# Splitting two contraction pairs of the down product before they are spilled, and loading their halves straight into place

## The chip, the cores and the metric

The kernel runs on one core of one Trainium2 chip. The metric is the device time of one execution in microseconds (us), the median of several runs. Engines are named as in the profile: PE is TensorE's matmul, DVE VectorE, ACT ScalarE, POOL GpSimd, and SP is the engine that issues all DMAs, in the order in which they stand in its queue.

## The reference

The model is a trunk of two layers over 1024 tokens of width 1024, in float32. The attention and recurrence half of a layer is not touched here. What matters is the MLP behind it (D_FF is 4096):

```python
        h2 = rms_norm(x, norm2_g[l])
        u = jax.nn.relu(jnp.einsum('bsd,df->bsf', h2, w_up[l]))
        x = x + jnp.einsum('bsf,fd->bsd', u * u, w_down[l])
```

Below, the first product is the up product, the second the down product. The down product contracts over the 4096 columns of u*u.

## The kernel before

PE takes operands in a rounded form of float32, so each operand X is split into a high part (ACT casts it, `split_into` L543 and `group` L595) and a low part (DVE subtracts the high part from X). A product of two operands is then three matmuls: low times high, high times low and high times high. One matmul of 128x512 outputs is the unit of PE's work.

Both products of the MLP use Strassen's scheme in Winograd's form. The hidden width of 4096 is cut into 16 pairs (of 256 columns each). For each pair the scheme needs seven right-hand **forms** (B11, B21, T2, T1, T3, B22, T4, in the order of FORMS, L541), and seven left-hand forms of the weights (A11, A12, S2, S1, S3, S4, A22), which `lhs_forms` (L578) makes from a loaded block `wr` (two buffers): POOL forms the sums (tile `wst`), ACT casts (`whi`) and DVE subtracts (`wlo`). `whi` and `wlo` have two buffers each, so a group of weights is cast only when PE is done with the group before the last.

**Up product.** Pairs 0 and 1 are computed by `up_plain`, before the Strassen forms of the input stand. The pairs 2 to 15 are computed by `up_pair` (L650), 84 matmuls each. The results of a pair (squared ReLUs u11, u12, u21, u22, in tiles `x4` to `x7`, which alternate with the parity of q) are turned into the seven down-product forms by `spill` (L695) and written to the DRAM tensor `us`, 256 KB a form. Three partial results (p1, p6, p5) leave PSUM by copies on ACT (`out`, L656); PE goes on accumulating in the same bank only behind such a copy.

**Down product.** It is worked off in steps (`steps`, L963). The first step takes output block 0 with pairs 0 and 1 (42 matmuls), the second block 1 with pair 0 and block 2 with pairs 0, 1, 2 (84 matmuls), then twelve steps follow that move over four pairs each (step r=0 takes pairs 0 to 3). `fetch` (L923) loads the forms of a pair from `us` into the staging tiles `uf` (4 buffers) and `us` (6 buffers) and splits them into the form tiles. Those form tiles are the ones that held the split input of the up product (`form_tiles`, L548): a form tile comes free when the last up pair, q=15, has gone through that form. After each product the step adds the PSUM bank to the residual `x` on DVE (L735), and for the bank "a" PE goes on only behind this add:

```python
                x = xt[2 * t + i][hf]
                with tc.high_priority():
                    V.tensor_tensor(x, ps[j, bk], x, op=ALU.add)
```

**Around the change.** In the pass q=15 the code loads the residual blocks b=0 to 3 (`load_x`, L931, 8 DMAs), prefetches four forms of pair 0 into `uf`, computes the pair, and then splits and fetches the 14 forms of pairs 0 and 1 (L944 to L950), ahead of q=15's own spill; the residual blocks 4 to 7 follow (L952), into the tiles that q=14 and q=15 have left. A scheduler sets the order of each engine's queue from the dependences, its own estimates and the `high_priority` blocks; the code's order is only its starting point.

Of the kernel before, what the change touches and what calls it, by code (L numbers as in the profile page):

```python
# [11 lines left out]
F32 = mybir.dt.float32  # L12
F32R = mybir.dt.float32r
# [7 lines left out]
P = 128  # L21
# [4 lines left out]
HALF = 512  # L26
NH = 4
FF = 4096
NF = FF // P
# [8 lines left out]
LAST = 2 * NH - 1  # L38
US = 6
UF = 4  # L40


@with_exitstack
def trunk(ctx, tc, x, norm1_g, w_in, lam_qk, attn_norm_g, lb_logits, hgrn_norm_g,
# [4 lines left out]
    dma = nc.sync.dma_start  # L49
# [15 lines left out]
    def half(pool, tag, bufs):  # L65
        return pool.tile([P, HALF], F32, tag=tag, name=tag, bufs=bufs)
# [471 lines left out]


    us = dram.tile([P, NF // 2, 7, HALF], F32, name="us")  # L540
    FORMS = ("B11", "B21", "T2", "T1", "T3", "B22", "T4")  # L541

    def split_into(hl, src):  # L543
        A.copy(hl[0], src)
        V.tensor_tensor(hl[1], src, hl[0].bitcast(F32), op=ALU.subtract)
        return hl

    def form_tiles(f, k, mp):  # L548
        if f == "B11":
            return h_tiles(k, 0)  # L550
        if f == "B21":
            return h_tiles(k + 4, 0)
        if f == "B22":
            return h_tiles(k + 4, 1)
        if f == "T1":
            return h_tiles(k, 1)
        return tuple(mp.tile([P, HALF], F32R, tag=f"{f}{k}{i}", name=f"{f}{k}{i}") for i in range(2))
# [137 lines left out]
    def spill(q, u, mp):  # L695
        u11, u12, u21, u22 = u
        t1, t2, t4 = (half(mp, "us", US) for _ in range(3))
        put = lambda f, t: dma(us[:, q, FORMS.index(f)], t)
        put("B11", u11)
        V.tensor_tensor(t1, u12, u11, op=ALU.subtract)  # L700
        put("T1", t1)
        put("B22", u22)
        V.tensor_tensor(t2, u22, t1, op=ALU.subtract)
        put("T2", t2)
        V.tensor_tensor(u12, u22, u12, op=ALU.subtract)
        put("T3", u12)
        put("B21", u21)
        V.tensor_tensor(t4, u21, t2, op=ALU.subtract)
        put("T4", t4)

    def fetch_rhs(q, mp, r, st, names, tag):

        for f in names:
            if st is not None:
                st[f] = half(mp, tag, UF if tag == "uf" else US)
                dma(st[f], us[:, q, FORMS.index(f)])

    def split_rhs(q, mp, r, st):
        for f in list(st):
            r[f] = split_into(form_tiles(f, q % 4, mp), st.pop(f))  # L720
# [35 lines left out]
    for l in range(DEPTH):  # L756
# [7 lines left out]
        for h in range(NH):  # L764
# [35 lines left out]
            st = {}  # L800
# [133 lines left out]
                dma(xt[b][hf], xs[:, b, hf * HALF:(hf + 1) * HALF])  # L934

        for q in range(2, NF // 2):
            if q == NF // 2 - 1:
                for b in range(4):
                    load_x(b)
                st = {}  # L940
                fetch_rhs(0, mp, None, st, FORMS[:UF], "uf")
            u2 = up_pair(up_forms(q, "AS2"), hB, q, xtile, mp)
            if q == NF // 2 - 1:
                for i in range(2):  # L944
                    uB[i] = {}
                    split_rhs(i, mp, uB[i], st)
                    fetch_rhs(i, mp, None, st, [f for f in FORMS if f not in uB[i]][:UF], "uf")
                    split_rhs(i, mp, uB[i], st)
                    if i == 0:
                        fetch_rhs(1, mp, None, st, FORMS[:UF], "uf")  # L950
            spill(q, u2, mp)
        for b in range(4, NB):  # L952
            load_x(b)
# [1 line left out]
        def down_forms(windows, parts):  # L955
            srcs = []
            for t, q0, n in windows:
                src = w_down[l][q0 * 256:(q0 + n) * 256, t * 256:t * 256 + 256]
                srcs.append(src.rearrange("(b p) d -> p b d", p=P))
            return lhs_forms(srcs, mp, "p (j i) c -> p i j c", parts)  # L960


# [54 lines left out]
```

## Time and profile before

| what | value |
|---|---|
| median of 3 runs | 2603.7 us (2601.36 to 2609.66) |
| profiled execution | 2602.21 us, its span 2600.2 us (2.0 us lie around the span) |
| PE busy | 2476.9 us, 95% of the span |
| DVE, ACT, POOL busy | 1837.1 (71%), 1260.4 (48%), 568.5 us (22%) |
| DMA | 306.86 MB, a mean of 118 GB/s; 0.4 to 0.5 of the 16 DMA engines busy in the MLP |

The span holds two layers; the MLP of the first lies from about 640 to 1265 us, that of the second from about 1930 to 2560 us. PE is nearly always busy, so what matters is where it is not: the stretches of a few us in which PE waits. The profile names for each such wait the engine that ended it.

### The profile page before, as it was taken

What the parts mean: (1) busy time and instruction counts of PE and PEld (TensorE: products, weight loads), DVE (VectorE), ACT (ScalarE), POOL (GpSimd) and SP (SyncE); (2) the same over time, 40 slices, a digit from 0 to 9 for tenths busy, and PEclk for the clock granted to TensorE, in tenths of its full rate; (3) what the DMA queues carried; (4) which work ended last, traced back from release to release, by engine and by line L of the source; (5) the groups of instructions that cost most, each with busy time, mean ns of one, the idle gap of its engine ahead of it and who ended that gap; (6) DMA issues with size and microseconds to landing.
All of it is one profiled execution on the core that took longest, in us unless ns stands there. A gap on an engine that the chain in (4) does not pass through costs nothing. (4 is left out here: it accounts for less than half of the span.)

```text
span 2600.2 us, 34936 instructions
## 1 busy us (share of the span) xinstructions
PE 2476.9 (95%) x12688; PEld 2053.2 (79%) x12688; DVE 1837.1 (71%) x3201; ACT 1260.4 (48%) x2439; POOL 568.5 (22%) x328
## 2 busy tenths in 40 slices
PE   8999999999999999999899999999999999899995
PEld 6877887777888877888688778877778888678874
DVE  5567756878756679877745875588786665887865
ACT  6455445654555554443434554456545555533422
POOL 1111011001133323333221111110012333233322
PEclk9999999999999999999999999999999999999998
DMA  7121111245444466453411111111645444754422
GB/s 228 52 61 45 46 37 53 74 141 176 154 154 150 142 214 199 147 162 97 154 49 49 41 37 53 50 41 58 218 129 173 153 155 142 251 159 147 156 85 89
DMA packets 255885, 306.86 MB, mean 118 GB/s; under 512 B 13968, under 2 KB 166844, under 8 KB 255712
## 3 DMA queue, kind: packets, MB, share of 16 engines
q1 hardware_dynamic: 255712, 304.63, 36.1%
q8 instruction: 100, 1.64, 0.3%
q14 instruction: 73, 0.60, 0.1%
HBM read 213.33 MB, written 89.41 MB: 116 GB/s over the span
## 5 line engine op out<-in xcount | busy, mean ns | idle before, releaser
L647 PE MATMUL pa<-T,whi 128*128 128x512 f32 x1456 | 459.1, 396 | 17.4 <-DVE x L735 12.1
L144 PE MATMUL mm<-hh,wlo 128*128 128x512 f32 x896 | 360.1, 402 | 1.7 <-POOL wlo L130 1.7
L144 PE MATMUL mm<-hh,whi 128*128 128x512 f32 x896 | 359.8, 402 | 1.0 <-DVE ta L772 0.9
L144 PE MATMUL mm<-hl,whi 128*128 128x512 f32 x896 | 359.2, 401 | 0.6 <-DVE hl L121 0.5
L647 PEld LDWEIGHTS pa<-T,whi 128*128 128x128 f32 x1456 | 273.1, 189 | 86.4 <-DVE x L735 7.5
L130 POOL TENSOR_TENSOR wlo<-wst,whi 128x1024 fp32r<-128x1024 f32 x56 | 138.9, 2480 | 807.1 <-ACT whi L128 771.4
L620 POOL TENSOR_TENSOR wst<-wr 128x512 f32<-128x512 f32 (+1 forms) x56 | 100.9, 1801 | 914.5 <-DMA wr<-w_down 293.6
L647 PE MATMUL pa<-T,wlo 128*128 128x512 f32 x728 | 287.0, 394 | 0.0
L606 ACT CAST whi<-wst 128x1024 fp32r<-128x1024 f32 (+1 forms) x124 | 127.1, 1025 | 175.8 <-PE mm L647 88.6
L607 DVE TENSOR_TENSOR wlo<-wst,whi 128x1024 fp32r<-128x1024 f32 (+1 forms) x124 | 192.7, 1554 | 14.9 <-ACT whi L606 14.6
L144 PEld LDWEIGHTS mm<-hh,wlo 128*128 128x128 f32 x896 | 170.6, 190 | 36.1 <-POOL wlo L130 4.0
L144 PEld LDWEIGHTS mm<-hl,whi 128*128 128x128 f32 x896 | 171.4, 191 | 33.6 <-DVE hl L121 1.7
L606 ACT CAST whi<-wr 128x512 fp32r<-128x512 f32 (+2 forms) x128 | 105.1, 821 | 189.4 <-PE pr L647 134.7
L144 PEld LDWEIGHTS mm<-hh,whi 128*128 128x128 f32 x896 | 170.7, 191 | 32.8 <-DVE ta L772 1.7
L647 PE MATMUL pr<-hh,whi 128*128 128x512 f32 x480 | 191.7, 400 | 3.6 <-ACT whi L606 3.1
L647 PE MATMUL pr<-hh,wlo 128*128 128x512 f32 x480 | 189.9, 396 | 0.9 <-DVE wlo L607 0.9
L647 PE MATMUL pr<-hl,whi 128*128 128x512 f32 x480 | 188.8, 393 | 0.0
L607 DVE TENSOR_TENSOR wlo<-wr,whi 128x512 fp32r<-128x512 f32 (+2 forms) x128 | 120.9, 945 | 86.3 <-ACT whi L606 84.2
L647 PEld LDWEIGHTS pa<-T,wlo 128*128 128x128 f32 x728 | 137.4, 189 | 33.2 <-DVE wlo L607 0.5
L512 ACT ACTIVATE s<-s,nm 128x256 f32<-128x256 f32 (+7 forms) x128 | 99.0, 774 | 109.2 <-DVE nm L507 105.0
L222 PE MATMUL mm<-wlo,hh 128*128 128x256 f32 x512 | 146.7, 287 | 0.3 <-POOL wlo L130 0.3
L222 PE MATMUL mm<-whi,hh 128*128 128x256 f32 x512 | 147.0, 287 | 0.0
(273 smaller groups left out, 5713.1 us busy)
## 6 DMA issues: line engine op xcount, KB each, us to landing
us<-us SPq DMA_DIRECT2D x216, 256.0 KB, 2.6
wr<-w_up SPq DMA_DIRECT2D x32, 1024.0 KB, 8.3
wst<-w_in SPq DMA_DIRECT2D x56, 512.0 KB, 3.7
uf<-us SPq DMA_DIRECT2D x112, 256.0 KB, 3.1
us<-x SPq DMA_DIRECT2D x112, 256.0 KB, 2.4
wr<-w_down SPq DMA_DIRECT2D x28, 1024.0 KB, 7.8
wst<-w_out SPq DMA_DIRECT2D x32, 512.0 KB, 4.7
x<-xs SPq DMA_DIRECT2D x64, 256.0 KB, 3.7
```

Of the source, the lines that this page charges most:

```text
L130: eng.tensor_tensor(lo, st, hi.bitcast(F32), op=ALU.subtract)
L144: T.matmul(ps, lt[:, b], rt, start=(i == 0), stop=(i == n - 1))
L222: T.matmul(ps[:, t * 256:t * 256 + 256], lt[:, tsl], rt[:, b], start=(i + t + b + k == 0), stop=(i == 1 and b == 3 and k == 2), skip_group ...
L512: A.activation(s[:, :nk], s[:, :nk], AF.Exp, bias=nm, scale=-1.0, accum_out=sm)
L606: A.copy(hv, x)
L607: V.tensor_tensor(lv, x, hv.bitcast(F32), op=ALU.subtract)
L620: G.tensor_tensor(sa[:, 0], a21, a22, op=ALU.add)
L647: T.matmul(ps, lt[:, off + j], rt, start=(start and j + i == 0), stop=(j == n - 1 and i == 2), skip_group_check=True)
```

## The change

- The pairs get **places**: pair q takes place (q - 2) mod 16 in the down product. So the down product begins with the pairs that `up_pair` computes first (q=2 and q=3, places 0 and 1), and the plain pairs 0 and 1 come last. `down_forms` loads the rows of `w_down` to match; where a window straddles the seam, it loads two pieces.
- For places 0 and 1 `spill` splits each form at once, into two `uf` tiles, and writes both halves to a new DRAM tensor `uss` (28 DMAs of 256 KB in place of 14).
- In the pass q=15 these 28 halves are loaded from `uss` straight into the form tiles; the prefetch into `uf` and the 14 splits there are gone.
- `load_x` for blocks 0 to 3 is written in the pass q=8 instead of q=15.

```diff
+READY = 2
...
     us = dram.tile([P, NF // 2, 7, HALF], F32, name="us")
+    uss = dram.tile([P, READY, 7, 2, HALF], F32, name="uss")
+
+    place = lambda q: (q - 2) % (NF // 2)
...
     def spill(q, u, mp):
         u11, u12, u21, u22 = u
         t1, t2, t4 = (half(mp, "us", US) for _ in range(3))
-        put = lambda f, t: dma(us[:, q, FORMS.index(f)], t)
+        p = place(q)
+
+        def put(f, t):
+            if p >= READY:
+                dma(us[:, p, FORMS.index(f)], t)
+                return
+            hl = [half(mp, "uf", UF) for _ in range(2)]
+            split_into([i.bitcast(F32R) for i in hl], t)
+            for i in range(2):
+                dma(uss[:, p, FORMS.index(f), i], hl[i])
+
         put("B11", u11)
...
         for q in range(2, NF // 2):
-            if q == NF // 2 - 1:
+            if q == 8:
                 for b in range(4):
                     load_x(b)
-                st = {}
-                fetch_rhs(0, mp, None, st, FORMS[:UF], "uf")
             u2 = up_pair(up_forms(q, "AS2"), hB, q, xtile, mp)
             if q == NF // 2 - 1:
-                for i in range(2):
+                for i in range(READY):
                     uB[i] = {}
-                    split_rhs(i, mp, uB[i], st)
-                    fetch_rhs(i, mp, None, st, [f for f in FORMS if f not in uB[i]][:UF], "uf")
-                    split_rhs(i, mp, uB[i], st)
-                    if i == 0:
-                        fetch_rhs(1, mp, None, st, FORMS[:UF], "uf")
+                for j, f in enumerate(FORMS):
+                    for i in range(READY):
+                        uB[i][f] = form_tiles(f, i, mp)
+                        for k in range(2):
+                            dma(uB[i][f][k].bitcast(F32), uss[:, i, j, k])
             spill(q, u2, mp)
...
             for t, q0, n in windows:
-                src = w_down[l][q0 * 256:(q0 + n) * 256, t * 256:t * 256 + 256]
-                srcs.append(src.rearrange("(b p) d -> p b d", p=P))
+                cut = min(n, max(NF // 2 - 2 - q0, 0))
+                for p0, m in ((q0, cut), (q0 + cut, n - cut)):
+                    if m:
+                        q = (p0 + 2) % (NF // 2)
+                        src = w_down[l][q * 256:(q + m) * 256, t * 256:t * 256 + 256]
+                        srcs.append(src.rearrange("(b p) d -> p b d", p=P))
```

The scheduler turns this into other queues at three places. Line numbers and tile numbers in what follows are each kernel's own.

**SP, start of the down product.** This is SP's queue from the weights of step r=0 (`wr`, 8x256) to the first load that fetches pair 2 into a `us` tile (B11; in the first layer). Before:

```order
L586 DMA wr_9222<-w_down 128x8x256
L698 DMA us_470<-x5_1_8720 128x512
L934 DMA x7_1_8931<-xs_111 128x512
L716 DMA uf_9039<-us_470 128x512
L716 DMA uf_9186<-us_470 128x512
L934 DMA x5_1_8923<-xs_111 128x512
L716 DMA us_9009<-us_470 128x512
```

After, the same queue from the last `uss` load of form B22 on (T4 is `T400` to `T411`):

```order
L962 DMA hl5_1_8935<-uss_471 128x512
L590 DMA wr_9265<-w_down 128x8x256
L962 DMA T400_8938<-uss_471 128x512
L962 DMA T401_8939<-uss_471 128x512
L962 DMA T410_8942<-uss_471 128x512
L962 DMA T411_8943<-uss_471 128x512
L706 DMA us_470<-x4_1_8782 128x512
L706 DMA us_470<-us_8946 128x512
L706 DMA us_470<-x7_1_8785 128x512
L706 DMA us_470<-us_8947 128x512
L706 DMA us_470<-x5_1_8783 128x512
L706 DMA us_470<-x6_1_8784 128x512
```

Then come the last spill of q=15 (`us_8948`), the eight residual loads of blocks 4 to 7, and only then B11 of pair 2:

```order
L706 DMA us_470<-us_8948 128x512
L948 DMA x4_0_8960<-xs_111 128x512
L948 DMA x4_1_8962<-xs_111 128x512
L948 DMA x5_0_8964<-xs_111 128x512
L948 DMA x5_1_8966<-xs_111 128x512
L948 DMA x6_0_8968<-xs_111 128x512
L948 DMA x6_1_8970<-xs_111 128x512
L948 DMA x7_0_8972<-xs_111 128x512
L948 DMA x7_1_8974<-xs_111 128x512
L730 DMA us_9052<-us_470 128x512
```

Between the weights of r=0 and pair 2's B11 stood 5 DMAs before; now there are 19: T4 of pairs 0 and 1 (4), the whole spill of q=15 (7) and the residual (8).

**PE, from step 1 to step 2.** Before, T4 of pairs 0 and 1 is the last product of step 1 (bank 8957), and step 2 begins behind it (banks 9076, 9079, 9077):

```order
L647 MATMUL pa_8957<-T410_8899,whi_8953 128x512
L647 MATMUL pa_8957<-T411_8900,whi_8953 128x512
L647 MATMUL pa_8957<-T410_8899,wlo_8954 128x512
L647 MATMUL pa_9076<-hh0_0_8827,whi_9054 128x512
L647 MATMUL pa_9076<-hl0_0_8828,whi_9054 128x512
```

After, T4 stands among the first products of step 2 (bank 9000 is step 1's), and ahead of B11 of pair 2 (`hh2_0`) lie pair 2's T1 and other forms that come from `uf`:

```order
L651 MATMUL pa_9000<-T411_8943,whi_8996 128x512
L651 MATMUL pa_9000<-T410_8942,wlo_8997 128x512
L651 MATMUL mm_9123<-hh6_0_9060,whi_9097 128x512
L651 MATMUL mm_9123<-hl6_0_9061,whi_9097 128x512
L651 MATMUL mm_9123<-hh6_0_9060,wlo_9098 128x512
L651 MATMUL pa_9119<-T200_8906,whi_9105 128x512
L651 MATMUL pa_9119<-T201_8907,whi_9105 128x512
```

From the first matmul of step 2 to B11 of pair 2 PE now has 42 matmuls (six of them T4), and from there to step r=0 another 48.

**SP, start of the up pairs.** Before, between the residual loads and the next weights (`wr`), with the prefetch of pair 0 into `uf`:

```order
L934 DMA x3_1_8685<-xs_111 128x512
L716 DMA uf_8687<-us_470 128x512
L698 DMA us_470<-x4_0_6797 128x512
L716 DMA uf_8689<-us_470 128x512
L716 DMA uf_8691<-us_470 128x512
L586 DMA wr_7065<-w_up 128x8x256
```

After, at the same place:

```order
L948 DMA x3_1_7734<-xs_111 128x512
L711 DMA uss_471<-uf_6909 128x512
L711 DMA uss_471<-uf_6910 128x512
L590 DMA wr_7136<-w_up 128x8x256
L711 DMA uss_471<-uf_6916 128x512
L711 DMA uss_471<-uf_6922 128x512
```

The eight loads of the residual blocks 0 to 3 (the last is `x3_1`) stand at the same place in both queues, ahead of the first spill of q=2; the spills of q=2 and q=3 go to `uss` in halves.

## Rows read from the trace of the kernel before

**Rows 1.** Page, head and part 1: span, and each engine's busy time.
```profile
span 2600.2 us, 34936 instructions
PE 2476.9 (95%) x12688; PEld 2053.2 (79%) x12688; DVE 1837.1 (71%) x3201; ACT 1260.4 (48%) x2439; POOL 568.5 (22%) x328
```

**Rows 2.** Timeline of PE, layer 0: start, length, instruction [idle before <- who ended it].
```profile
954.99 0.40 PE L647 MATMUL pa<-hh,whi 128*128 128x512 f32 x1
...
960.02 0.71 PE L647 MATMUL pa<-T,whi 128*128 128x512 f32 x2 [2.10 <-DVE x L735]
...
964.14 0.79 PE L647 MATMUL pa<-T,whi 128*128 128x512 f32 x1 [1.24 <-DVE T L545]
...
979.13 0.50 PE L647 MATMUL mm<-hl,whi 128*128 128x512 f32 x1 [1.91 <-DVE hl L545]
...
994.14 0.40 PE L647 MATMUL pa<-hh,whi 128*128 128x512 f32 x1
...
1007.33 0.71 PE L647 MATMUL pa<-T,whi 128*128 128x512 f32 x2 [2.00 <-DVE x L735]
```

**Rows 3.** The same view, layer 1: steps 1 and r=0 begin, waits in r=0.
```profile
2231.99 0.40 PE L647 MATMUL pa<-hh,whi 128*128 128x512 f32 x1
...
2272.87 0.40 PE L647 MATMUL pa<-hh,whi 128*128 128x512 f32 x1
...
2278.88 0.71 PE L647 MATMUL pa<-T,whi 128*128 128x512 f32 x2 [0.36 <-DVE x L735]
...
2285.86 0.70 PE L647 MATMUL pa<-T,whi 128*128 128x512 f32 x2 [1.22 <-DVE x L735]
```

**Rows 4.** Stretches: length, busy (x count) of PE, PEld, DVE, ACT, POOL, PEclk, DMA, GB/s.
```profile
704.00:724.00 20.00, 20.00 (x88) 16.31 (x88) 12.65 (x12) 10.87 (x16) 7.01 (x6) 1.00 0.42 145
960.00:965.00 5.00, 3.74 (x10) 2.42 (x11) 5.00 (x6) 0.28 (x1) 2.99 (x2) 0.62 0.48 164
2560.00:2565.00 5.00, 4.55 (x20) 4.16 (x21) 2.86 (x9) 1.10 (x3) 1.27 (x1) 0.50 0.08 30
606.00:612.00 6.00, 6.00 (x29) 4.95 (x28) 6.00 (x10) 3.73 (x6) 0.00 (x0) 1.00 1.01 329
688.00:692.00 4.00, 4.00 (x19) 3.11 (x18) 3.24 (x5) 1.54 (x2) 0.00 (x0) 1.00 1.02 380
```

**Rows 5.** Timeline of SP: weights of step r=0, in layer 0 and layer 1.
```profile
967.34 0.38 SPq L586 DMA_DIRECT2D wr<-w_down  x1
...
2243.67 0.38 SPq L586 DMA_DIRECT2D wr<-w_down  x1
```

**Rows 6.** Timelines of DVE and ACT, layer 0: step 1's last weights; first cast from `us`.
```profile
966.86 0.41 DVE L607 TENSOR_TENSOR wlo<-wr,whi 128x256 fp32r<-128x256 f32 x1
...
978.78 0.62 ACT L544 CAST hh<-us 128x512 fp32r<-128x512 f32 x1 [1.78 <-DMA us<-us]
```

**Rows 7.** Instructions on tile `us` (ns min/median/max); weights' cast and DMA landing, from the page.
```profile
L544 ACT CAST T<-us x84: 613/618/627, 983.7 to 2505.1; 128x512 fp32r<-128x512 f32 x84
L545 DVE TENSOR_TENSOR T<-us,T x84: 676/692/1810, 985.8 to 2506.4; 128x512 fp32r<-128x512 f32 x84
L606 ACT CAST whi<-wst 128x1024 fp32r<-128x1024 f32 (+1 forms) x124 | 127.1, 1025 | 175.8 <-PE mm L647 88.6
us<-us SPq DMA_DIRECT2D x216, 256.0 KB, 2.6
```

**Rows 8.** Timeline of PE at the kernel's end: a long wait.
```profile
2559.54 1.86 PE L195 MATMUL pa<-ones,us 128*128 128x1 f32 x8 [11.30 <-DVE us L187]
```

**Rows 9.** Timeline of SP, layer 0: the first residual loads, first and last line of 8 loads.
```profile
667.81 4.17 SPq L934 DMA_DIRECT2D x<-xs  x4
...
690.82 0.54 SPq L934 DMA_DIRECT2D x<-xs  x1
```

**Rows 10.** Pair q=3 in the up product: ACT's copy of p6, PE's next use of that bank.
```profile
712.28 0.59 ACT L659 COPY us<-pa 128x512 f32<-128x512 f32 x1 [0.67 <-PE pa L647]
...
714.85 0.63 PE L647 MATMUL pa<-T,whi 128*128 128x512 f32 x2
```

## The prediction

> **What bounds the kernel now.** First the page's head: PE is busy for 2476.9 of 2600.2 us [rows 1], so only a stretch in which PE waits can give time back, and any new wait of PE is paid in full. Then the timeline of PE, searched for entries with an idle time. The up product has none (from 704 to 724 us PE is busy for 20.00 of 20 [rows 4]); they lie in a cluster at the passage to the down product. There I measure from the start of step 1, T0 = 954.99 us in layer 0 and 2231.99 in layer 1. Step r=0 begins at 994.14 and 2272.87 [rows 2, 3], that is T0+39.2 and T0+40.9. Steps 1 and 2 are 126 matmuls; at full clock PE does 88 in 20.00 us [rows 4], 0.227 us each, so 28.6 us would do. The passage thus loses 10.6 and 12.3 us, and r=0 another 2.00 and 0.36 + 1.22 us [rows 2, 3]. About 26 us in all is what the change can win at most.
>
> Who ends the waits? The first (2.10 us) and those of r=0 are ended by DVE's add of a bank to the residual; the next (1.24 and 1.91 us) by DVE's low parts of right-hand forms [rows 2]. Part of the loss is the clock: from 960 to 965 the granted clock is 0.62 [rows 4].
>
> **What the change takes away.** 28 operations at each passage: 14 casts of 0.62 us on ACT and 14 subtractions of 0.69 us on DVE [rows 7]. DVE's 9.7 us lie in the stretch where DVE ends PE's waits, so 1.24 and 1.91 us can go in layer 0. The first wait stays: the order keeps q=15's own subtractions and step 1's low parts ahead of the first add, and only one split goes from before it. I leave it at 4.6 to 5.0 us after T0.
>
> **What it adds in the up product.** The 28 split operations come back in the passes q=3 and q=4, about 4.3 us of ACT and 4.8 of DVE in each pair's 19.3 us. DVE is busy for 12.65 and ACT for 10.87 of 20 us there [rows 4], so they fit. The risk is order: a form goes through two of four `uf` tiles, so each cast waits on ACT for the landing of the form two before (2.6 us from issue [rows 7]), and ACT's copy of p6 stands behind such casts. The copy ends at 712.87 and PE takes the bank at 714.85 [rows 10], 1.98 us of cover. Going through ACT's new order with the durations of rows 7, the copy ends about 1.7 us later: just covered. I charge 0.25 us for each of four pairs, 1.0 in all (bounds 0 and 12). The 14 more writes per layer, 0.7 us each, fall where the DMA share is 0.42 [rows 4] and cost nothing; without that cover they would cost up to 10 us a layer. The five more pieces of `w_down` per layer hide in the same way.
>
> **The residual.** Its first eight loads run from 667.81 to 690.82 [rows 9], before q=2, already now; the queue of the changed kernel has them at the same place. This part of the change moves nothing: 0 us. It can gain nothing at the passage because it is not there.
>
> **What it adds at the passage.** This decides. 28 loads of 256 KB replace 14, four of which were taken early, and all run through SP's one queue. The order puts the weights of r=0 ahead of the T4 loads, and behind these the whole spill of q=15, the eight other residual loads and only then B11 of pair 2, which step 2 needs. SP holds everything behind a waiting instruction, so I follow this queue:
>
> 1. The weights of r=0 wait for the buffer that step 1 leaves, that is for DVE's last low part of step 1 (966.86 + 0.41 us [rows 6]; SP issues at 967.34 [rows 5]). That is T0+12.4 and T0+11.7 (2243.67). Without the 1.24 us wait and its neighbours, at full clock, it would be: restart at 4.6, twelve matmuls 2.7, add 0.7, low part 0.4, issue and handshakes 0.6: T0+9.0. At half clock add about 1. I take T0+9.5 (bounds 9.0 and 12.4).
> 2. From there to pair 2's B11 lie 1 MB of weights and 20 loads or writes of 256 KB, 6.29 MB. Weights, in rows of 1 KB, run at 329 GB/s with all DMA engines busy, forms, in rows of 2 KB, at 380 [rows 4]: 3.2 us + 20 x 0.69 = 17.0, and 1.9 more for one transfer's landing (2.6 us less its own 0.69) [rows 7], 18.9 us. From the other side: before, with 5 transfers between, the first cast from `us` began 11.4 us after the weights' issue (978.78 less 967.34 [rows 5, 6]); 14 more at 0.69 make 21.1. I take 20: B11 lands at T0+29.5.
> 3. By then PE has long done the 42 matmuls that stand before it and waits, by this count some 6 to 7 us. After B11 (three matmuls) PE needs S3, whose cast stands on ACT behind three casts of forms (0.62 us each) and takes 1.03 us [rows 7]: T0+32.5. Then 45 matmuls at 0.227, 10.2 us, to r=0.
> 4. After a wait of this size the clock is low: behind the 11.30 us wait at the kernel's end the granted clock is 0.50 for the next 5 us [rows 4, 8]. Two or three of these us pass while ACT casts; I charge 1.5 us (bounds 0 and 3).
>
> So r=0 begins at T0+44.2 instead of 39.2 and 40.9: +5.0 and +3.3 us. In r=0 DVE's splits of pair 3 are then mostly done; I let half of the 3.6 us of waits there go, -1.8. With 0.5 us for handshakes in step 2 that no row prices (bounds 0 and 4) and 1.0 in the up product the sum is 5.0 + 3.3 - 1.8 + 0.5 + 1.0 = **+8.0 us**; on the profiled execution's 2602.2 us (its span of 2600.2 [rows 1] and 2.0 around it) that makes 2610.2. The median of the runs, 2603.7, lies 1.5 us above that execution, so I give **2611.7**. That is +0.3%, about what a measurement of this kernel can tell from no change (0.3%, 7.8 us).
>
> The one rule of the Trainium skill that speaks the other way: "DMA: Bandwidth & Descriptors", section Bandwidth, gives a fabric ceiling of 435 GB/s. By it an estimate for 6.29 MB is 14.5 us instead of 17.0, and the sum would be 5 us lower, +3.0. The trace does not bear that out for such transfers: 380 GB/s at a full share [rows 4].
>
> **Rivals.**
>
> *The loads keep up (faster).* If pair 2's B11 landed before PE asks for it, the passage would keep only the first add's wait (about 2 us), the casts between steps (about 3) and r=0's. PE reaches B11 near T0+22.5 (step 1 to T0+11, a cast, 42 matmuls of 9.5 us, another cast). The point from which it decides: 6.29 MB in 22.5 - 9.5 - 1.9 = 11 us, 570 GB/s, or an issue of the weights 7 us sooner. r=0 would begin near T0+34: -5 and -7 us, with r=0's half -1.8, 2590. For it: ACT and DVE are relieved exactly where PE waits for DVE. Against it: no stretch in rows 4 is near 570 GB/s, and the order is fixed.
>
> *The staging in the up product throttles (slower still).* If a landing among the w_up transfers takes 4.6 us instead of 2.6, two landings in ACT's way delay p6's copy by 4 us more, against a cover already used up: 3 to 4 us in each of four pairs, 12 to 16 in all, 2620 to 2625. For it: ACT executes in order and the cover is 1.98 us. Against it: SP has no other large transfer in those microseconds.
>
> *Nothing to see.* The early residual moves nothing, and the splits' saving (1.24 + 1.91 us with the clock, some 4 to 5 us a layer) pays for the later B11: 2600 to 2607. For it: the queue without any gap would deliver B11 at about T0+26.5, r=0 near T0+41.
>
> **How the numbers follow.** Forecast 0.62, faster rival 0.11, staging 0.14, nothing to see 0.13. The forecast's own range, 2604 to 2619, has the bound of 0.3% in its middle, so it gives half to slower and half to within. Slower: 0.31 + 0.14 = 0.45. Within 0.3%: 0.31 + 0.13 = 0.44. Faster: 0.11. The range, 2599 to 2622, leaves out the faster rival and the upper part of the staging rival.
>
> **What would show it.** Right: at the passage PE's longest wait is no longer DVE's low part but ends with a cast of pair 2's B11 (`hh` from `us`, behind a DMA) and lasts 5 to 9 us in each layer; the weights of r=0 issue near T0+9.5; r=0 begins near T0+44; the up product shows no new wait above 0.5 us; the first eight residual loads are where they were. Wrong: no wait over 3 us in step 2, r=0 before T0+39, or PE idle behind ACT's copies in q=3 and q=4.

## The result and the profile after

Over five runs of each on one chip the changed kernel took 2621.5 us (median) against 2603.7: 1.0073 times as long, 95% interval 1.0047 to 1.0100. A second set (experiment 7 below) gave 2625.5 against 2607.1, 1.0078 (1.0059 to 1.0097). It is slower by about 18 us, where +8.0 us was forecast.

The profiled execution of the changed kernel is the slowest of its five runs, 2630.8 us. The page's head, to compare with [rows 1]:

```profile
span 2629.0 us, 35049 instructions
...
PE 2493.0 (95%) x12688; PEld 2065.9 (79%) x12688; DVE 1831.7 (70%) x3201; ACT 1258.2 (48%) x2439; POOL 567.0 (22%) x328
```

The number of matmuls is the same, and the operations of DVE and ACT too: the splits were moved, not removed. The span grew by 28.8 us, but not all of that is the change's. SP's timeline shows the first spills of the up product, up to which the code is untouched; first the kernel before, then the changed one (start, length, instruction, count):

```profile
652.11 14.22 SPq L698 DMA_DIRECT2D us<-uf  x4
```

```profile
662.57 14.22 SPq L706 DMA_DIRECT2D us<-uf  x4
```

10.5 us were lost ahead of the first changed instruction. In the 17 profiles of this study that row starts anywhere between 650.3 and 662.8, so single profiles are compared stage by stage: the *up product* from the end of this row to T0, and the *passage* from T0 to step r=0. (Expectations below count the up product from the row's start, 302.9 us before; as the row itself lasts from 14.2 to 16.4 us, the measured figures are from its end, 288.7 and 288.8 us before.)

**The passage.** PE's timeline, layer 0 from T0 to r=0, then layer 1, to compare with [rows 2, 3]:

```profile
968.51 0.40 PE L651 MATMUL pa<-hh,whi 128*128 128x512 f32 x1
...
972.62 0.70 PE L651 MATMUL pa<-T,whi 128*128 128x512 f32 x2 [1.17 <-ACT whi L610]
...
999.34 0.80 PE L651 MATMUL pa<-hh,whi 128*128 128x512 f32 x1 [6.90 <-ACT hh L548]
...
1002.05 1.65 PE L651 MATMUL pa<-T,whi 128*128 128x512 f32 x3 [0.76 <-ACT whi L610]
...
1014.60 0.39 PE L651 MATMUL pa<-hh,whi 128*128 128x512 f32 x1
...
2258.15 0.40 PE L651 MATMUL pa<-hh,whi 128*128 128x512 f32 x1
...
2288.42 0.79 PE L651 MATMUL pa<-hh,whi 128*128 128x512 f32 x1 [5.84 <-ACT hh L548]
...
2304.22 0.39 PE L651 MATMUL pa<-hh,whi 128*128 128x512 f32 x1
```

The waits that DVE's low parts ended are gone. In their place PE waits 6.90 and 5.84 us for the high half of pair 2's B11. r=0 begins at T0+46.1 in both layers, 6.9 and 5.2 us later than before. In r=0 the waits of 2.00 and 0.36 + 1.22 us [rows 2, 3] are gone. SP's timeline shows why B11 is late (the last load ahead of the weights of r=0, the weights, the residual, pair 2), to compare with [rows 5]:

```profile
971.04 0.32 SPq L962 DMA_DIRECT2D hl<-uss  x1
977.55 0.38 SPq L590 DMA_DIRECT2D wr<-w_down  x1
...
987.02 5.95 SPq L948 DMA_DIRECT2D x<-xs  x8
993.01 3.97 SPq L730 DMA_DIRECT2D us<-us  x6
```

SP issues nothing from 971.36 to 977.55, in front of the weights. They go at T0+9.0, and pair 2's first load goes 15.5 us after them, behind the T4 loads, the spill and eight residual loads. The stretches of the passage (length; busy time of PE, PEld, DVE, ACT, POOL; PEclk, DMA share, GB/s), and one of the up product where splits now are:

```profile
968.50:973.50 5.00, 3.83 (x17) 2.85 (x16) 4.93 (x5) 2.41 (x5) 4.30 (x4) 1.00 1.05 395
...
998.50:1003.50 5.00, 3.40 (x7) 1.97 (x8) 4.11 (x6) 4.41 (x8) 0.00 (x0) 0.50 0.99 352
...
722.60:742.60 20.00, 18.50 (x81) 14.80 (x80) 15.79 (x19) 13.76 (x22) 4.93 (x3) 1.00 0.71 237
```

Behind the long wait the granted clock is 0.50, that is 1.2 GHz. And **the up product**, which had no wait at all, now has one of 1.0 to 1.7 us in each of the two pairs with splits: it takes 291.7 and 292.5 us, 3.1 and 3.7 more. PE's timeline has the wait; ACT's, DVE's and GpSimd's (the next three fences) have its cause; the last two fences are DVE's and GpSimd's rows of the same place in the kernel before:

```profile
727.03 0.74 PE L651 MATMUL pa<-T,whi 128*128 128x512 f32 x2 [1.50 <-ACT us L663]
```

```profile
723.72 0.63 ACT L696 ACTIVATE x<-x 128x512 f32<-128x512 f32 x1 [2.47 <-DVE x L695]
724.25 0.61 ACT L548 CAST uf<-x 128x512 fp32r<-128x512 f32 x1
724.76 0.63 ACT L697 ACTIVATE x<-x 128x512 f32<-128x512 f32 x1
725.87 0.62 ACT L548 CAST uf<-x 128x512 fp32r<-128x512 f32 x1 [0.48 <-DMA uss<-uf]
726.40 0.58 ACT L663 COPY us<-pa 128x512 f32<-128x512 f32 x1
```

```profile
718.96 0.68 DVE L549 TENSOR_TENSOR uf<-us,uf 128x512 fp32r<-128x512 f32 x1
719.57 1.80 DVE L722 TENSOR_TENSOR us<-x,us 128x512 f32<-128x512 f32 x1
721.29 1.79 DVE L549 TENSOR_TENSOR uf<-x,uf 128x512 fp32r<-128x512 f32 x1
723.00 0.68 DVE L695 TENSOR_TENSOR x<-mm,us 128x512 f32<-128x512 f32 x1
```

```profile
719.12 1.70 POOL L596 TENSOR_TENSOR wst<-wr 128x512 f32<-128x512 f32 x1 [2.36 <-DVE wlo L611]
720.78 1.75 POOL L596 TENSOR_TENSOR wst<-wr,wst 128x512 f32<-128x512 f32 x1
```

```profile
708.45 0.68 DVE L708 TENSOR_TENSOR us<-x,us 128x512 f32<-128x512 f32 x1
709.59 0.69 DVE L691 TENSOR_TENSOR x<-mm,us 128x512 f32<-128x512 f32 x1 [0.47 <-PE mm L647]
```

```profile
708.60 1.70 POOL L592 TENSOR_TENSOR wst<-wr 128x512 f32<-128x512 f32 x1 [2.36 <-DVE wlo L607]
```

Start with DVE. It has two of the added subtractions (L549, 0.68 and 1.79 us) ahead of the add L695, and the spill's own subtraction between them (L722, L708 before) takes 1.80 us beside GpSimd's sums, 0.68 before. So the add starts 60.43 us after the first spill; before it was 57.48, and DVE was waiting for PE. ACT's relu (L696) waits 2.47 us for that add. Behind it, in order, come a cast, the square, a cast that waits 0.48 us for a landing, and only then the copy of p6 that frees PE's bank. That landing too stands behind DVE: it is of the low half that the subtraction of 1.79 us made, whose write SP issues at 723.52. So two paths lead from the added subtractions to the copy. The copy starts at 726.40, 63.83 us after the first spill; before it was 60.17 (712.28 [rows 10] less 652.11). That is 3.7 us later against a cover of 1.98.

By the stages of this profile: 3.1 + 3.7 us in the up products, 6.9 + 5.2 in the passages, about 3.5 back in the steps r=0, +15.4 us together. The measured difference is 17.8 (12 to 26).

### The profile page after: what moved, and what is told of

It reads as the page before. It is cut to its first block, busy times and chain, and to the rows that moved or that the text cites. A ratio compares the mean times of both kernels' runs of the same rounds, so it can differ in the third digit from the quotient of the medians.

```text
span 2629.0 us, 35049 instructions
## 1 busy us (share of the span) xinstructions
PE 2493.0 (95%) x12688; PEld 2065.9 (79%) x12688; DVE 1831.7 (70%) x3201; ACT 1258.2 (48%) x2439; POOL 567.0 (22%) x328
```

## The experiments

Each run's time is set against runs of the kernel before on the same chip; the table at the end has all stages. The diffs are against the changed kernel, cut where "..." stands. Three questions: which parts cost anything, why the passage is longer, why the up product is.

**1. Everything but the split.** Rotated places and early residual loads only:

```diff
-            hl = [half(mp, "uf", UF) for _ in range(2)]
-            split_into([i.bitcast(F32R) for i in hl], t)
...
+        put = lambda f, t: dma(us[:, p, FORMS.index(f)], t)
...
-                for j, f in enumerate(FORMS):
-                    for i in range(READY):
-                        uB[i][f] = form_tiles(f, i, mp)
-                        for k in range(2):
-                            dma(uB[i][f][k].bitcast(F32), uss[:, i, j, k])
+                for i in range(2):
+                    uB[i] = {}
+                    split_rhs(i, mp, uB[i], st)
...
```

> This kernel has the rotated places and the early residual loads of the change, and none of the split forms: spill, early fetch and splits stand as in the kernel before. Theory A (the change costs time in two places: about 6.7 us by the splits that were added to the up product, and about 8.6 us in the passage from the up product to the step r = 0, with the relief in r = 0 taken off): these two parts cost nothing, so within 3 us of the kernel before (2601 to 2607). Rival C (rotated places and the weights that come in two pieces cost something themselves): 2610 to 2618. Theory B (all in the passage) agrees with A here.

1.0005 (0.9989 to 1.0022): no cost, and every stage is within 0.6 us of before. The residual and the rotation are off the list; theory C falls.

**2. The splits in the up product alone.**

```diff
-                dma(st[f], us[:, q, FORMS.index(f)])
+                dma(st[f], uss[:, q, FORMS.index(f), 0] if q < READY else us[:, q, FORMS.index(f)])
...
-                for j, f in enumerate(FORMS):
-                    for i in range(READY):
-                        uB[i][f] = form_tiles(f, i, mp)
-                        for k in range(2):
-                            dma(uB[i][f][k].bitcast(F32), uss[:, i, j, k])
+                for i in range(2):
+                    uB[i] = {}
+                    split_rhs(i, mp, uB[i], st)
...
```

> The forms of the first two places are split amid the up product and go out in two halves, as in the change; the passage is that of the kernel before, which loads one tile per form and splits it (it loads the high half alone, so the low half is left out of the result). Theory A: about 6.7 us above the kernel before, 2607 to 2614. Theory B (the later up product in the trace of the change is drift from run to run, as the 10 us ahead of the up product are, and all of the cost lies in the passage): within 3 us of the kernel before, 2601 to 2607.

1.0021 (1.0004 to 1.0038), 5.5 us; the up products take 291.6 and 290.9 us, the passages 38.5 and 38.8. The cost is in the up product, as theory A has it; B would need 0.

**3. The passage alone.**

```diff
-            split_into([i.bitcast(F32R) for i in hl], t)
...
+        put = lambda f, t: dma(us[:, p, FORMS.index(f)], t)
...
-                            dma(uB[i][f][k].bitcast(F32), uss[:, i, j, k])
+                            dma(uB[i][f][k].bitcast(F32), us[:, i, j])
```

> The forms go out unsplit as in the kernel before, and the passage is that of the change: 28 loads into place and no splits (high and low tile are both loaded from the same unsplit form, so the split is left out of the result). Theory A: 12.1 us more in the two passages, 3.5 us less in the two steps r = 0: 2609 to 2616, with the wait for pair 2's form B11 at 6 to 7 us in each layer. Theory B: the whole loss of the change, 2617 to 2624.

1.0032 (1.0017 to 1.0047), 8.4 us. The up products are back at 288.5 and 288.8 us, the passages are 45.0 and 44.4, and the waits for B11 are 6.73 and 5.94 us. Theory A: two separate prices, which add up to 13.9 us.

**4. Pair 2's first forms ahead of the 28 loads.**

```diff
-                    st = {}
-                    fetch_rhs(i, mp, uB[i], st, [f], "uf" if j % 2 else "us")
+                    st = {f: ahead.pop(f)} if i == READY and f in ahead else {}
+                    if not st:
+                        fetch_rhs(i, mp, uB[i], st, [f], "uf" if j % 2 else "us")
...
+            if q == NF // 2 - 1:
+                ahead = {}
+                fetch_rhs(READY, mp, None, ahead, FORMS[:UF], "uf")
```

> The change as it is, but the first four forms of pair 2 are loaded at the last pair of the up product into the four uf tiles, ahead of the 28 loads, instead of six us loads after the residual. Theory A with the queue's order as cause of the wait: the wait for B11 of pair 2 (6.9 and 5.8 us) goes and with it the half clock behind it (about 3 us a layer); another, shorter wait on T3 of pair 2 or on the 28 loads, which start 3 us later, takes 2 to 4 us a layer: 2604 to 2612. Rival D (bytes decide: the same megabytes must land before r = 0, whichever goes first): the wait moves to another form and stays as long, 2616 to 2624.

1.0033 (1.0017 to 1.0048), 2615.2 us, between the figures of the two theories. The long wait is gone, and in layer 0 no stretch of the passage has a granted clock under 1.00; r=0 begins at T0+40.0 and 42.0. But ten waits of 0.2 to 2.1 us on loads, casts, adds and low parts stand in each passage, and nothing is won against the kernel before. The place in the queue made the one long wait; the rest of it is spread over others.

**5. Half of the loads.**

```diff
-                        uB[i][f] = form_tiles(f, i, mp)
-                        for k in range(2):
-                            dma(uB[i][f][k].bitcast(F32), uss[:, i, j, k])
+                        uB[i][f] = form_tiles(f, i, mp)[:1] * 2
+                        dma(uB[i][f][0].bitcast(F32), uss[:, i, j, 0])
```

> The change, but only the high half of the first two pairs is loaded and used for both products (14 loads instead of 28; the low halves are left out of the result). Theory A (the 28 loads and what stands behind them in the queue make B11 of pair 2 late): 14 loads less at 0.69 us each bring it 9.7 us earlier, so its wait of 6.9 and 5.8 us and the half clock behind it go; r = 0 at 37 to 40 us from T0 instead of 46.1, the run at 2602 to 2609. Rival E (ScalarE's cast of B11 waits for its tile or its place, not for the load): the wait stays over 5 us and the run at 2614 to 2622.

0.9986 (0.9968 to 1.0004), although its up products are as long as the change's (291.7 and 291.5 us). SP's timeline (the weights of r=0, pair 2) and PE's wait for B11:

```profile
978.59 0.38 SPq L590 DMA_DIRECT2D wr<-w_down  x1
...
981.94 5.78 SPq L730 DMA_DIRECT2D us<-us  x6
```

```profile
990.33 0.50 PE L651 MATMUL pa<-hh,whi 128*128 128x512 f32 x1 [0.63 <-ACT hh L548]
```

T0 is 969.39 here: pair 2's first load goes at T0+12.6 instead of T0+24.5. The wait falls from 6.90 to 0.63 us and r=0 begins at T0+33.6 and 34.1, 12 us earlier and earlier than theory A had it. This passage is even 5.5 and 6.8 us shorter than the kernel before's. Rival E falls. But the loads left out are not the only difference. The weights of r=0 go at nearly the same time (T0+9.2, in the change T0+9.0), and of the 14 loads only two stood behind them in the change. What moved most is the order: the scheduler now has T4, the whole spill of q=15 and three residual loads ahead of the weights, where in the change SP stood still for 6.2 us, and only five loads lie between the weights and pair 2. So the run shows that this passage without splits on DVE and ACT can be shorter than before, and not what 14 loads cost. In all three kernels of experiment 12 the spill stands ahead of these weights too.

**6. Four residual loads behind pair 2.**

```diff
-        for b in range(4, NB):
+        for b in range(4, 6):
             load_x(b)
...
+            if ws is steps[1]:
+                for b in range(6, NB):
+                    load_x(b)
```

> The change, but the residual's blocks 6 and 7 (four loads) are loaded behind the forms of pair 2. Theory A (the place in the queue, one load after the other at 0.69 us): B11 of pair 2 lands 2.8 us earlier, PE waits 4.1 and 3.0 us for it instead of 6.9 and 5.8, r = 0 at 42.5 to 44 us from T0 instead of 46.1: the run 4 to 7 us under the change, 2612 to 2618. Rival E (the cast waits for something else): no difference, 2616 to 2624.

1.0046 (1.0029 to 1.0063), 12 us over before, 6 us under the median of the change on the same chip; the 2619.4 us lie just above theory A's range. The waits for B11 are 3.30 and 2.96 us, r=0 at T0+43.1 and 41.6: place in the queue, as theory A says. Against the change on the same chip (experiment 7) the four loads were worth 3.7 and 3.1 us of the passage.

**7. The change again**, beside experiments 6, 10 and 11:

> The change again, on the chip of the runs beside it. By the sum of its stages (6.5 us in the up products, 12 us in the passages, 3.5 us back in the steps r = 0): 15 us over the kernel before, 2615 to 2623, with up products of 305 to 307 us, r = 0 at 45 to 47 us from T0 and waits of 5.5 to 7 us for B11 of pair 2. If the time ahead of the up product was part of the change's effect, the first spill is again 10 us later than before (662 instead of 652); if it was drift, it is anywhere between 651 and 663.

1.0078 and 2625.5 us, a little above the range; up products 291.6 and 291.6 us, r=0 at T0+46.8 and 44.7. The waits for B11 are 4.04 and 5.55 us; the first is shorter than expected, as more of that passage's loss lies in other waits (1.24 us of it for one of the 28 loads). The first spill was at 662.8 again. Whether that is chance can't be told from two profiles; it was also 662.1 in experiment 5 and 653.3 in experiment 2, whose up products have the same splits.

**8. Eight tiles for the halves.** Now to the up product. If landings hold back the casts, more tiles should help:

```diff
-            hl = [half(mp, "uf", UF) for _ in range(2)]
+            hl = [xtile(stage[0] % 4, i) for i in range(2)]
+            stage[0] += 1
...
```

> The change with the split halves of the first two places in eight tiles of their own (those of the residual's blocks 0 to 3, which are loaded only when they are free) instead of the four uf tiles, so that no cast waits for a spill to land. Theory S1 (the added subtractions stand in VectorE's queue ahead of the add that the next evacuation needs): the up products stay at 305 to 307 us (302.9 before) and the run at 2615 to 2623. Theory S2 (the casts wait for the landing of the halves): the up products fall to 303 to 304 us and the run to 2610 to 2616.

1.0090 (1.0070 to 1.0110), 23.5 us. The up products take 295.2 and 296.0 us, worse than the change's. No cast waits for a landing any more, but the queues have another order: a cast in front of the copy of p1 waits 2.83 us for DVE, and PE waits 2.35 us behind that copy. S2 falls; S1 had forecast no change, not such a loss. Why the order came out so is not shown.

**9. Splits spread over pairs 5 to 11.** Forms go out unsplit, and in each of these pairs `restage` loads two, casts and subtracts them and writes the halves out:

```diff
+            if 5 <= q < 5 + len(FORMS):
+                for i in range(READY):
+                    restage(i, FORMS[q - 5], mp)
...
```

> The change, but the first two places go out unsplit; in each of the pairs 5 to 11 of the up product two of their forms are loaded, split and written out, so two splits a pair instead of seven in pairs 2 and 3 (and 14 loads more). Theory S1 or S2 (the crowd of splits in two pairs): up products of 303 to 304 us, the run 5 to 6 us under the change: 2610 to 2617. Rival S3 (each split costs its share wherever it stands): up products stay at 305 to 307 us, 2615 to 2623.

1.0096 (1.0076 to 1.0117); up products 294.2 and 294.5 us. ACT's timeline ahead of the longest of layer 0's four waits:

```profile
743.18 0.62 ACT L720 CAST uf<-uf 128x512 fp32r<-128x512 f32 x1 [2.73 <-DMA uf<-us]
743.70 0.58 ACT L663 COPY us<-pa 128x512 f32<-128x512 f32 x1
```

Fewer splits a pair, but each may stand right in front of the copy and wait there for its own load. S3 comes nearest, and falls short by 5 us (2627.9 us against at most 2623). With **one place only** (same spreading, READY = 1, the second pair split in the passage):

> Only the first place goes out split (one form in each of the pairs 5 to 11), and is loaded into place by 14 loads; the second is loaded early into the uf tiles and split as in the kernel before. Theory A (loads beyond what lands behind the two first steps cost, splits beyond what VectorE gets done in them cost): half of each fits, r = 0 at 36 to 39 us from T0 (38.9 and 40.9 before) and no wait over 2 us: 2594 to 2603. Rival F (each load of a split form costs as much as the split it saves): 2603 to 2612.

1.0023 (1.0009 to 1.0038): up products 292.2 and 293.1 us for seven splits, passages 39.8 and 38.0. The time is rival F's, though not by its reason alone: the up products cost 3.6 and 4.4 us more than before, and the passages give 2.2 us back.

**10. Casts on GpSimd.**

```diff
-            split_into([i.bitcast(F32R) for i in hl], t)
+            G.tensor_copy(hl[0].bitcast(F32R), t)
+            V.tensor_tensor(hl[1].bitcast(F32R), t, hl[0], op=ALU.subtract)
```

> The change, but the 14 high halves that the up product makes for the first two places are cast on GpSimd instead of ScalarE; the 14 subtractions stay on VectorE. Theory S4 (a cast that waits, for a landing, for VectorE or for a form's load, stands in ScalarE's queue ahead of the copy of p6 that frees the bank for the next product): with no cast in that queue the up products fall from 305.9 and 306.7 us to 303 to 304 and the run to 2609 to 2615. Theory S1 (VectorE's backlog alone delays the adds): they stay at 305 to 307 us, the run at 2615 to 2623. Rival G (GpSimd, which makes the weights' sums, becomes late with them, and slows VectorE beside it): over 307 us.

1.0106 (1.0087 to 1.0124), up products 298.0 and 298.6 us: the longest of all. None of the 14 casts is left in ACT's queue, and still ACT's copy is late. ACT's timeline, then DVE's, then GpSimd's:

```profile
721.60 0.63 ACT L696 ACTIVATE x<-x 128x512 f32<-128x512 f32 x1 [5.43 <-DVE x L695]
...
722.79 0.57 ACT L663 COPY us<-pa 128x512 f32<-128x512 f32 x1
```

```profile
715.88 1.80 DVE L720 TENSOR_TENSOR x<-x,x 128x512 f32<-128x512 f32 x1
717.61 1.79 DVE L723 TENSOR_TENSOR us<-x,us 128x512 f32<-128x512 f32 x1
719.90 1.06 DVE L710 TENSOR_TENSOR uf<-us,uf 128x512 fp32r<-128x512 f32 x1 [0.50 <-POOL uf L709]
720.89 0.68 DVE L695 TENSOR_TENSOR x<-mm,us 128x512 f32<-128x512 f32 x1
```

```profile
715.44 1.69 POOL L596 TENSOR_TENSOR wst<-wr 128x512 f32<-128x512 f32 x1 [1.76 <-DVE wlo L611]
717.09 1.76 POOL L596 TENSOR_TENSOR wst<-wr,wst 128x512 f32<-128x512 f32 x1
718.80 1.07 POOL L709 CAST uf<-us 128x512 fp32r<-128x512 f32 x1
```

The relu waits 5.43 us for the add. DVE is late with it because subtractions ahead of it wait for GpSimd's casts (0.50 us) and run 1.8 us beside GpSimd's sums. Rival G holds. S4 alone would have had the price go; but since DVE is slowed here, this run does not tell S4 from S1, and experiment 11 does.

**11. No subtractions.** This kernel leaves out DVE's share of the splits and nothing else:

```diff
-            split_into([i.bitcast(F32R) for i in hl], t)
+            A.copy(hl[0].bitcast(F32R), t)
             for i in range(2):
-                dma(uss[:, p, FORMS.index(f), i], hl[i])
+                dma(uss[:, p, FORMS.index(f), i], hl[0])
```

> The change without the 14 subtractions of a layer that make the low halves in the up product (the high half is written in both places, so the low half is left out of the result); its casts, tiles and spills stay. Theory S1 (VectorE's added subtractions delay the add L695, ScalarE waits for it, and the copy of p6 stands behind): up products of 303 to 304 us instead of 305.8 to 306.7, the run 4 to 6 us under the change. Theory S4 (casts that wait for landings in ScalarE's queue): they stay at 305 us or more, and the run within 3 us of the change.

1.0031 (1.0016 to 1.0047), 8.1 us over before; by the ratios that is 11 us under the change, of which the up products show 6. They take 288.7 and 289.1 us, as before the change, where S4 had them stay long: the added subtractions are what costs. ACT's rows at the same place, and DVE's row of the add:

```profile
714.30 0.63 ACT L696 ACTIVATE x<-x 128x512 f32<-128x512 f32 x1
714.84 0.61 ACT L709 CAST uf<-us 128x512 fp32r<-128x512 f32 x1
715.35 0.62 ACT L697 ACTIVATE x<-x 128x512 f32<-128x512 f32 x1
716.27 0.59 ACT L663 COPY us<-pa 128x512 f32<-128x512 f32 x1 [0.29 <-PE pa L651]
```

```profile
713.57 0.69 DVE L695 TENSOR_TENSOR x<-mm,us 128x512 f32<-128x512 f32 x1 [0.47 <-PE mm L651]
```

All 14 casts are still in ACT's queue, one between the relu and the square as in the change. But the add now waits for PE, the relu for nothing, and the copy for PE's bank. The cast that in the change waited for a landing in front of the copy now stands behind it. So both paths of the change, through the add and through the landing, are gone with the subtractions; which of the two costs how much, no run separates.

**12. Towards a kernel that beats both.** One place split ahead, the residual's blocks 6 and 7 behind pair 2 (as in 6), in three ways: casts on GpSimd, casts on ScalarE, and one form a pair, paced by a tile that the rotation of the pair itself sets free.

> One place alone goes out split (its seven casts on GpSimd), the second is split in the passage as in the kernel before, and the residual's blocks 6 and 7 are loaded behind the forms of pair 2 instead of ahead of them. If the casts in ScalarE's queue and the loads ahead of pair 2 were what cost: up products of 303 to 304 us, r = 0 at 36 to 38 us from T0 (38.9 and 40.9 before), the run at 2596 to 2602, under the kernel before. If a split form's loads give back what they save: 2603 to 2610.

0.9984 (0.9969 to 0.9999): r=0 at T0+35.1 and 34.9, but the up products take 293.3 us each (casts on GpSimd), so by these stages almost all is given back.

> The kernel with one place split ahead and the residual's blocks 6 and 7 behind pair 2, but its seven casts on ScalarE as in the change, not on GpSimd. If the price goes with the number of splits: up products of 304 to 305 us (half of the 3.1 us of the change; 307.5 with the casts on GpSimd), passages of 35 us as there, the run 4 to 7 us under that with GpSimd's casts: 2592 to 2599. If the first split already costs the whole wait: up products of 306 us, 2597 to 2604.

0.9977 (0.9961 to 0.9992): up products 290.3 and 290.7 us, about half of the change's price for half of its splits.

```diff
...
+            if 4 <= q <= 4 + len(FORMS):
+                if q > 4:
+                    restage(FORMS[q - 5], held, mp)
+                if q < 4 + len(FORMS):
+                    held = half(mp, "us", US)
+                    dma(held, us[:, 0, q - 4])
...
```

> One place split ahead, one form in each of the pairs 5 to 11: the form is loaded into a us tile, which the rotation gives it only when the pair before has let go of it, and is cast and subtracted one pair later; the passage as in the last one. If one added cast and one added subtraction a pair fit into the slack of the queues (ScalarE waited 1.95 us for a bank ahead of the copies of p5 and p6 in the kernel before): up products of 302.9 to 303.7 us, passages of 35 us, the run at 2588 to 2597, some 10 us under the kernel before. If the cast waits for its load or its turn: 304.5 us or more, 2595 to 2604.

0.9966 (0.9951 to 0.9981): 2598.1 us against 2605.7, 8.9 us faster by the ratio (5 to 13), just above the range expected. The up products take 289.4 and 288.7 us. PE's timeline of layer 0's passage, whole in its waits:

```profile
965.39 0.40 PE L651 MATMUL pa<-hh,whi 128*128 128x512 f32 x1
...
970.60 1.09 PE L651 MATMUL pa<-T,whi 128*128 128x512 f32 x2 [2.27 <-issue]
...
986.91 0.50 PE L651 MATMUL pa<-hl,whi 128*128 128x512 f32 x1 [0.28 <-DVE hl L549]
...
988.61 0.50 PE L651 MATMUL mm<-hl,whi 128*128 128x512 f32 x1 [0.74 <-DVE hl L549]
...
1000.39 0.40 PE L651 MATMUL pa<-hh,whi 128*128 128x512 f32 x1
```

r=0 begins at T0+35.0 in both layers, 4.2 and 5.9 us earlier than in the kernel before: half of the splits are off DVE's path, only half of the extra loads are in the queue, and only four loads lie between the weights of r=0 and pair 2's first load.

| kernel | up product, layers 0 and 1 | T0 to r=0 | time by before (interval) |
|---|---|---|---|
| before | 288.7, 288.8 | 39.2, 40.9 | 1 |
| the change | 291.7, 292.5 | 46.1, 46.1 | 1.0073 (1.0047, 1.0100) |
| the change again (7) | 291.6, 291.6 | 46.8, 44.7 | 1.0078 (1.0059, 1.0097) |
| rotation and residual only (1) | 288.6, 288.8 | 38.6, 41.0 | 1.0005 (0.9989, 1.0022) |
| splits only (2) | 291.6, 290.9 | 38.5, 38.8 | 1.0021 (1.0004, 1.0038) |
| passage only (3) | 288.5, 288.8 | 45.0, 44.4 | 1.0032 (1.0017, 1.0047) |
| early pair 2 (4) | 291.6, 292.2 | 40.0, 42.0 | 1.0033 (1.0017, 1.0048) |
| half of the loads (5) | 291.7, 291.5 | 33.6, 34.1 | 0.9986 (0.9968, 1.0004) |
| late residual (6) | 291.6, 291.6 | 43.1, 41.6 | 1.0046 (1.0029, 1.0063) |
| eight tiles (8) | 295.2, 296.0 | 46.2, 44.4 | 1.0090 (1.0070, 1.0110) |
| spread (9) | 294.2, 294.5 | 45.6, 45.5 | 1.0096 (1.0076, 1.0117) |
| spread, one place (9) | 292.2, 293.1 | 39.8, 38.0 | 1.0023 (1.0009, 1.0038) |
| casts on GpSimd (10) | 298.0, 298.6 | 45.7, 45.3 | 1.0106 (1.0087, 1.0124) |
| no subtractions (11) | 288.7, 289.1 | 47.1, 46.5 | 1.0031 (1.0016, 1.0047) |
| one place, GpSimd (12) | 293.3, 293.3 | 35.1, 34.9 | 0.9984 (0.9969, 0.9999) |
| one place, ScalarE (12) | 290.3, 290.7 | 35.4, 36.1 | 0.9977 (0.9961, 0.9992) |
| one place, paced (12) | 289.4, 288.7 | 35.0, 35.0 | 0.9966 (0.9951, 0.9981) |

## Why the prediction was wrong in size

The direction and the place held: slower, through the loads at the passage. The time, 2621.5, lies at the upper edge of the range. The sum said +8.0 and the stages of the profile say +15.4: the up products are 5.8 us above their term and the passages 3.8 us, the relief in r=0 is 1.7 us larger than forecast, and the 0.5 us for handshakes are already in the measured passages.

*The term of the up product failed: "I charge 0.25 us for each of four pairs, 1.0 in all".* It was 5.8 to 6.8 us in the profiles of the change, 5.5 by the run with the splits alone. The step put only landings in ACT's way and let the copy of p6 come 1.7 us later, inside a cover of 1.98. It came 3.7 us later, because DVE's new subtractions stand ahead of the add on which ACT's queue waits, and ahead of the landing on which its last cast waits; without them the price is gone (experiment 11). That "they fit" by busy time (12.65 of 20 us) was true and beside the point: DVE had 15.79 of 20 us in that stretch, and what mattered was which instruction stood ahead of which. One of the two subtractions also took 1.79 us, not the 0.69 that the step charged, beside a sum of GpSimd's; rows 7 have that case as well, in their longest, 1.810 us. The rival "staging throttles" named the right place, but its mechanism, longer landings, is not what was seen (the casts in front of the copy wait 0.48 us for one, and experiment 8 removes such waits and loses more); its price was two to three times the measured one.

*The passage was right in its steps, short at its end.* The weights of r=0 went at T0+9.0 and 9.8 (forecast 9.5). PE waited 6.9 and 5.8 us (6 to 7). S3's matmul went at T0+33.5 and 33.0 (32.5). From there to r=0 it took 12.6 and 13.1 us where 45 matmuls at full clock are 10.2: the half clock cost 2.4 and 2.9 us after S3 against 1.5 charged, near its bound of 3. So r=0 began at T0+46.1 instead of 44.2, and the two passages cost 12.1 us instead of 8.3. That the place in the queue made this wait, experiments 4 and 6 show; in experiment 5 the number of loads and the order changed together.

*The relief in r=0 was too small.* All of the 3.6 us of waits went, not half.

*The residual moves nothing*: right. In the changed profile its loads start at 678.27, 15.7 us after the first spill, 667.81 before [rows 9] also 15.7; experiment 1 has it at no cost, with the rotation.

*The rival "the loads keep up"* was rightly held unlikely: a stretch of 5 us of the passage moved 406 GB/s at most (2279.10 to 2284.10), where that rival asked for 570. The Trainium skill's ceiling of 435 GB/s ("DMA: Bandwidth & Descriptors", section Bandwidth) was not reached here either. But its other half, that ACT and DVE are relieved where PE waits for DVE, is borne out: with half of the loads, and the spill ahead of the weights, the passage was 6 us shorter than in the kernel before.

Open: the stages give 13.7 to 15.4 us, the runs' medians about 18, with intervals that reach down to 12 and 15. The rest would lie in stretches whose code is the same, which differ by several us between any two profiles; no run here separates it. Not tried: a second queue for the loads, or all 28 loads with the spill ahead of the weights of r=0, as the scheduler placed it in experiment 5.

## What to carry to other kernels

Moving work into a stage where PE never waits is not free because the engines have idle time: find the copy that frees PE's bank, list what the changed queues put ahead of it and ahead of what it waits for, and price each by its slow case. Splitting a spilled operand ahead of time doubles the bytes to be loaded back; look at what that does to the order of the one queue, and above all at what comes to stand behind an entry that waits for a buffer: here that was the spill, the residual and the first load that the next step needed. Background work cost least here when it was paced by a tile that the foreground frees once per round, one cast and one subtraction at a time (experiment 12 against 9); more buffers for it made it worse (experiment 8).

## What was not expected of the hardware

A subtraction of 128x512 on VectorE took 0.68 us alone, 1.06 to 1.07 when it began during one of GpSimd's casts, and 1.79 us when it began during one of GpSimd's sums of 1.6 to 1.8 us (the rows in the result and in experiment 10); begun 0.15 us ahead of such a sum it still took 0.68 (708.45 in the kernel before). GpSimd's cast, too, took 1.07 us beside such a subtraction and 0.61 elsewhere. The Trainium skill's "SBUF — State Buffer", section "SBUF: two separate sides", says that VectorE with two SBUF inputs and GpSimd lock a shared port for a whole instruction; the rows agree. Moving the casts to the idle engine cost more than leaving them where they were: up products of 298 us against 292.

Waits of like length were followed by different clocks. With eight tiles PE waited 2.35 us until 714.19 and 2.29 us until 736.04; the granted clock of the next 2 us was 1.00 behind the first, and behind the second 0.61, that is mostly 1.2 GHz:

```profile
714.20:716.20 2.00, 2.00 (x9) 1.65 (x10) 2.00 (x4) 1.35 (x3) 0.00 (x0) 1.00 0.33 126
736.20:738.20 2.00, 2.00 (x6) 1.59 (x7) 2.00 (x4) 1.34 (x3) 0.00 (x0) 0.61 0.42 154
```
